# A two-layer diffusion backbone on one core: gate product ahead of the reciprocal, narrower ones in the values, earlier projection blocks, modulation inside attention

## The chip, the cores and the metric

One core of one Trainium2 chip. The time is device microseconds of one execution; the table below gives the median of three runs and the one execution that the hardware profiler took.

## The reference

Two layers over 1024 latent tokens with a prefix of 256 context tokens, model width 1024, all in fp32. Each layer computes a modulation (shift, scale, gate) from a conditioning vector, an RMS norm, one input projection, two parallel mixers with SiLU gates, and one output projection:

```python
def modulation(cond, w, b):
    m = jax.nn.silu(cond) @ w + b
    return jnp.split(m, 3, axis=-1)
...
    for i in range(DEPTH):
        sh_l, sc_l, g_l = modulation(c, mod_w[i], mod_b[i])
        sh_c, sc_c, g_c = modulation(c_ctx, mod_w[i], mod_b[i])
        h_lat = rms_norm(x_lat, norm_g[i]) * (1.0 + sc_l[:, None, :]) + sh_l[:, None, :]
        h_ctx = rms_norm(x_ctx, norm_g[i]) * (1.0 + sc_c) + sh_c
        if i % 2 == 0:
            y_lat, y_ctx = even_mixer(h_lat, h_ctx, ...)   # A: global GQA, B: GQA in a band with a sink
        else:
            y_lat, y_ctx = odd_mixer(h_lat, h_ctx, ...)    # C: conformer convolution, D: 2-D neighbourhood attention
        x_lat = x_lat + g_l[:, None, :] * y_lat
        ...
    return rms_norm(x_lat, final_g)
```

In attention the softmax is followed by the gate: `oa * silu(ag)`, and the same for B and D.

## The kernel before

**Numbers and engines.** Every fp32 operand of a large product is split into a high part (ScalarE cast, line 325) and a low part (the rest, on GpSimd or VectorE, line 328), and a product is three matmuls (lines 347 to 349). TensorE is PE in the profile, VectorE DVE, ScalarE ACT, GpSimd POOL, and SP issues most DMAs.

**Order.** The code emits instructions with priorities, and a scheduler that simulates a timeline sets each engine's order from them. `later(n)` lowers the priority of what is emitted inside it; `issue_after(i)` queues the block's instructions behind `i` on the engine of `i`. `weave(main, n, fill, m)` takes n steps of attention and m of a filling generator in turn.

**Opening.** The string `PLAN` orders it: modulation halves of layer 0 (`a`, `b`, `c` on PE, `v` on DVE), loads of the three token chunks (`0`, `1`, `2`; 256 context tokens, then 512 and 512), sums of squares (`n`), the norm's factor (`r`) and the normalised, modulated and split chunk (`h`, the function `make_h`: line 335 on DVE, lines 338 to 342 on ACT, then the low part on DVE, line 339, or POOL, line 328). After it `fill0(0, w0)` projects the first head group: ten blocks j of 128 tokens with 384 columns (tile `pq`), two to a pair jp, rotary embedding per block (lines 855 to 860), transposes (`qk_tail`, tile `trk`), then three gate blocks (`pg`). The third chunk's norm is woven in at the blocks that `LASTN` names: its sum of squares (`norm_x`, line 726) at block 0, its factor (`norm_bc`, tile `trs`) at block 2, its `h` at block 3. During the opening the flag `solo` is set and the fillers' banks in PSUM (`pp`) come from two tags until `sums` is set, then from one tag with two banks.

**The other modulation halves.** Eight halves of 512 columns are left after `PLAN` (the generator `mod_steps`): the gate part of layer 0 and all of layer 1. A half has nine steps: eight, in each of which 128 rows of the weight are loaded and summed, weighted, on DVE for one or two conditioning vectors (lines 242 and 247; three rows of the second vector go to ACT and POOL), and one that ends it (lines 253 to 258). The first `PSH` halves sum in PSUM (tile `mrun`), the others in SBUF (`macc`). `tick()`, called three times in each projection block, takes one step: at every call while `solo` is set (`TICK0`), then at every third (`TICK1`). While `solo` is set the weights land in the tiles that later hold keys and values (tags KA, KB and V).

**Attention, layer 0.** Four head groups u in the order 2, 3 (B), 0, 1 (A), each in ten query blocks of 128 (a "group" in the code). For a key tile of 128: scores (tile `st`, two banks, lines 503 and 507), exponential (ACT, line 515, tile `pf`, `PFB` = 2 buffers under the tag `ost`), split into `ph` and `pl`, and three tiles later the products with the values (tile `ov`, one bank, lines 445 to 447). The value tile holds for a key tile 64 columns of the low part, 64 of the high part and 64 ones; the ones put the denominator into partitions 64 to 127 of `ov`. A group's end is lines 454 to 459: two transposes of the denominators, the reciprocal, a transpose back, and `finish`: numerators times reciprocals out of PSUM (line 669 in layer 0, 1451 in layer 1), then 0.5 and the gate (671, 1453). The next group's first product needs the bank `ov` and so waits for line 669. Row maxima for the group after next (`mx`, lines 614 to 635) run in between.

While group k runs, the projection of group k+1 fills. In the last one (u = 1) the output projection fills (`out0_part`, tile `po`): first the four features of u = 2, 3, then the two of u = 0, each part with its own accumulation in PSUM and its own addition to x (line 1090). `through_attention` then does the last features.

**Layer 1** has the same attention loop with 16 groups of seven tiles (exponential buffers under the tag `pf`, also `PFB`), beside projections and the output projection. The convolution before it is bound to DVE's line 1200.

## Time and profile before

| | |
|---|---|
| median of 3 runs | 1506.44 us (1504.36 to 1511.38) |
| profiled execution | 1513.41 us, span in the profile 1511.6 us |
| PE busy, granted clock | 1427.4 us, 94% of the span; 0.978 |
| DVE, POOL, ACT busy | 1086.5, 815.9, 750.7 us |
| DMA | 215 MB, mean 142 GB/s |

In a row of the grouped view stand line, engine, operation, output and inputs, shape and count; then the busy time, the mean of one in ns, and the idle time of that engine just before them with what ended it. A matmul's end is modelled, so that two that follow closely overlap in the list; the distance from start to start is the rate.

### The profile page before, as it was taken

The numbers are of one execution on the slowest core, as the hardware profiler recorded it, in microseconds if no ns is written. First come the engines' busy times: TensorE is split into PE (matmuls) and PEld (weight loads), VectorE is DVE, ScalarE is ACT, GpSimd is POOL, SyncE is SP. The second block draws the span as 40 slices with busy tenths as digits, with TensorE's granted clock in tenths as the row PEclk, the third lists the DMA queues.
The fourth block names the chain that finished last, engine by engine and source line by source line (L and its number), as shares of the span: only waits on it lengthen the run. The fifth ranks groups of instructions, "written<-read, shape, count | busy, mean of one in ns | idle before, by whom it ended". The sixth has DMA issues, their size and how long they took to land.

```text
span 1511.6 us, 22035 instructions
## 1 busy us (share of the span) xinstructions
PE 1427.4 (94%) x7006; PEld 1162.7 (77%) x7006; DVE 1086.5 (72%) x2139; ACT 750.7 (50%) x1536; POOL 815.9 (54%) x764
## 2 busy tenths in 40 slices
PE   7699999999999999999999989999999999999996
PEld 2598988887788678778888768888887778777775
DVE  4996787588957677555577686999838467667766
ACT  3541444445453765665455665443444354645563
POOL 3262463466555686776455765754543253354663
PEclk9799999999999999999999989999999999999998
DMA  9766245423541124641111122213596777786523
GB/s 350 260 198 194 70 122 179 143 70 115 159 136 48 45 84 120 221 157 38 49 42 43 60 91 66 92 58 80 164 308 189 206 228 207 249 273 209 190 63 119
DMA packets 182828, 215.24 MB, mean 142 GB/s; under 512 B 17196, under 2 KB 136184, under 8 KB 182712
## 3 DMA queue, kind: packets, MB, share of 16 engines
q1 hardware_dynamic: 172464, 195.97, 41.5%
q10 hardware_dynamic: 10248, 17.87, 3.7%
q8 instruction: 55, 0.90, 0.2%
q14 instruction: 61, 0.50, 0.1%
HBM read 151.64 MB, written 62.13 MB: 141 GB/s over the span
## 4 chain that ended last, share of the span: by engine, by line
PE 68%; DVE 13%; DMA 10%; issue 3%; POOL 2%; SPq 1%; ACT 1%; DVEq 0%; ACTq 0%; POOLq 0%
PE p L347 5%; PE p L348 5%; PE p L349 5%; PE ov L445 4%; PE ov L447 4%; PE ov L446 4%; PE po L347 4%; PE po L349 4%; PE po L348 4%; PE st L507 4%; PE st L503 4%; PE pg L347 2%; PE pg L349 2%; PE pg L348 2%; DMA mw<-in_mod_w_dram 2%
## 5 line engine op out<-in xcount | busy, mean ns | idle before, releaser
L328 POOL TENSOR_TENSOR pl<-pf,ph 128x512 fp32r<-128x512 f32 (+3 forms) x321 | 391.6, 1230 | 263.4 <-ACT ph L325 223.1
L328 POOL TENSOR_TENSOR wl<-wr,wh 128x256 fp32r<-128x256 f32 (+2 forms) x253 | 194.9, 789 | 157.5 <-ACT wh L325 114.6
L515 ACT ACTIVATE pf<-st 128x512 f32<-128x512 f32 x284 | 166.9, 596 | 178.4 <-PE st L507 125.6
L325 ACT CAST ph<-pf 128x512 fp32r<-128x512 f32 (+3 forms) x364 | 206.2, 578 | 25.4 <-PE ov L446 12.7
L347 PE MATMUL p<-hh,wh 128*128 128x512 f32 x448 | 177.9, 399 | 4.8 <-ACT wh L325 3.7
L348 PE MATMUL p<-hl,wh 128*128 128x512 f32 x448 | 178.3, 399 | 0.0
L349 PE MATMUL p<-hh,wl 128*128 128x512 f32 x448 | 173.3, 397 | 0.0
L325 ACT CAST wh<-wr 128x256 fp32r<-128x256 f32 (+2 forms) x260 | 102.0, 404 | 122.8 <-DMA wr<-in_od_d_dram 36.3
L445 PE MATMUL ov<-ph,Vt 128*128 128x512 f32 (+3 forms) x364 | 140.6, 386 | 9.5 <-DVE y L669 6.8
L503 PE MATMUL st<-QH,KAt 128*128 128x512 f32 (+3 forms) x364 | 140.3, 386 | 7.5 <-ACT pf L515 4.3
L447 PE MATMUL ov<-pl,Vt 128*128 128x512 f32 (+3 forms) x364 | 141.6, 391 | 4.9 <-POOL pl L328 3.0
L446 PE MATMUL ov<-ph,Vt 128*64 128x512 f32 (+3 forms) x364 | 138.1, 379 | 0.0
L507 PE MATMUL st<-QL,KBt 68*128 68x512 f32 (+3 forms) x364 | 135.1, 381 | 0.3 <-DVE QL L416 0.3
L1200 DVE SCALAR_TENSOR_TENSOR cps<-U,taps,cps 128x512 f32<-128x512 f32 x184 | 124.3, 749 | 0.1
L627 DVE TENSOR_REDUCE mp<-mx 128x1 f32<-128x512 f32 x128 | 85.6, 685 | 38.6 <-PE mx L626 37.9
L347 PEld LDWEIGHTS p<-hh,wh 128*128 128x128 f32 x448 | 84.6, 189 | 25.6 <-ACT wh L325 4.7
L349 PEld LDWEIGHTS p<-hh,wl 128*128 128x128 f32 x448 | 84.4, 189 | 19.7 <-issue 0.5
L348 PEld LDWEIGHTS p<-hl,wh 128*128 128x128 f32 x448 | 84.6, 189 | 18.9 <-issue 0.2
L447 PEld LDWEIGHTS ov<-pl,Vt 128*128 128x128 f32 x364 | 70.3, 193 | 29.5 <-POOL pl L328 7.8
L445 PEld LDWEIGHTS ov<-ph,Vt 128*128 128x128 f32 x364 | 70.7, 194 | 25.1 <-issue 5.3
L503 PEld LDWEIGHTS st<-QH,KAt 128*128 128x128 f32 x364 | 69.1, 190 | 26.3 <-ACT pf L515 10.3
L347 PE MATMUL pq<-wh,hh 128*128 128x384 f32 x256 | 88.7, 346 | 0.0
(289 smaller groups left out, 3463.5 us busy)
## 6 DMA issues: line engine op xcount, KB each, us to landing
mw<-in_mod_w_dram SPq DMA_DIRECT2D x34, 512.0 KB, 6.0
Q<-qs SPq DMA_DIRECT2D x40, 256.0 KB, 2.6
QH<-Q SPq DMA_DIRECT2D x80, 128.0 KB, 2.8
bm<-in_d_bm_dram SPq DMA_DIRECT2D x16, 540.0 KB, 5.9
wr<-in_od_d_dram SPq DMA_DIRECT2D x64, 128.0 KB, 2.9
mw<-in_mod_w_dram SPq DMA_DIRECT2D x28, 256.0 KB, 3.1
wr<-in_ev_qkv_dram SPq DMA_DIRECT2D x32, 192.0 KB, 4.5
QD<-spq SPq DMA_DIRECT2D x48, 128.0 KB, 2.5
```

The costliest lines, as they stand in the source:

```text
L325: SC.copy(hi, src)
L328: (GP if leng == "g" else VE).tensor_tensor(lo, src, hi.bitcast(F32), op=ALU.subtract)
L347: PE.matmul(o, lh, rh, start=first, stop=False)
L348: PE.matmul(o, lh, rl, start=False, stop=False)
L349: done[0] = PE.matmul(o, ll, rh, start=False, stop=last)
L445: PE.matmul(o, V[:, 64:192], ph, start=(t == 0), stop=False)
L446: PE.matmul(cut(g.ov[0:64], q0, n), V[:, 0:64], ph, start=False, stop=False)
L447: pvs.append(PE.matmul(o, V[:, 64:192], pl, start=False, stop=(last and g.sink is None)))
L503: sts.append(PE.matmul(sf, KA[:, cs], cut(g.QH, q0, n), start=True, stop=False))
L507: PE.matmul(sf, KB[0:68, cs], cut(g.QL[0:68], q0, n), start=False, stop=True)
L515: SC.activation(pf[:, :n], st[:, :n], AF.Exp, scale=1.0 if g.bias else SCALE)
L1200: VE.scalar_tensor_tensor(pc, uc, w, pc, op0=ALU.mult, op1=ALU.add)
```

## The change

- **Group ends.** A new `pre` runs after the two transposes and before the reciprocal: numerator x 0.5 x gate out of PSUM, in two instructions. `finish` multiplies the result by the reciprocals in SBUF.
- **Ones and buffers.** A value tile has 161 columns for a key tile, not 192: 33 ones. The first product of a group still takes 128 columns of weights, the others 97. `PFB` is 3 in both layers.
- **Opening.** `PLAN` gets `q` (blocks 0 and 1 of the first projection, copied to the tile `pc0`) and `n` (the third chunk's sum of squares) ahead of the second chunk's `h`. That sum is halved between POOL and DVE. `LASTN` is (2, 2, 3), with nothing left for the first entry.
- **Modulation.** Ticks count only from block 4; in the opening a step is queued behind the last line 339. `PSH` is 3. `TICK1` is 8, 6 and 16 for the first three head groups. The steps that are left run in u = 1, one at every fifth step of attention from the tenth, in the spare key and value buffers, all sums on DVE.
- **Output projection.** The features of u = 2, 3 and 0 are one part with one accumulation; `O1` is (6, 134, 14).

```diff
-PFB = 2
+VW = 161
+PFB = 3
-PSH = 4
+PSH = 3
-O1 = (6, 84, 46, 14)
-TICK0, TICK1 = (1, 3)
-PLAN = 'pavaa0vabvnabbvabrbbwcVHcccw1Ch2nrh'
-LASTN = (0, 2, 3)
+O1 = (6, 134, 14)
+TICK0, TICK1 = (1, (8, 6, 16))
+PLAN = 'pavaa0vabvnabbvabrbbwcVHcccw1Ch2nrqnh'
+LASTN = (2, 2, 3)
...
+    def new_v(pool, n, bufs):
+        V = pool.tile([P, n * VW + 192 - VW], F32R, tag="V", name=nm("Vt"), bufs=bufs)
+        for k in range(n):
+            GP.memset(V[:, k * VW + P : (k + 1) * VW].bitcast(F32), 1.0)
+        GP.memset(V[:, n * VW :].bitcast(F32), 1.0)
+        return V
...
-            PE.matmul(o, V[:, 64:192], ph, start=(t == 0), stop=False)
-            PE.matmul(cut(g.ov[0:64], q0, n), V[:, 0:64], ph, start=False, stop=False)
-            pvs.append(PE.matmul(o, V[:, 64:192], pl, start=False, stop=(last and g.sink is None)))
+            m = P if t == 0 else VW - 64
+            PE.matmul(o[0:m], V[:, vo + 64 : vo + 64 + m], ph, start=(t == 0), stop=False)
+            PE.matmul(cut(g.ov[0:64], q0, n), V[:, vo : vo + 64], ph, start=False, stop=False)
+            pvs.append(PE.matmul(o[0 : VW - 64], V[:, vo + 64 : vo + VW], pl, start=False, stop=(last and g.sink is None)))
...
+                yu = g.pre(g.ov)
                 VE.reciprocal(r8, r1[:, :, 0])
                 VE.transpose(rb, r8[:, :, None].broadcast_to([P, 8, 32]))
-                g.finish(g.ov, rb)
+                g.finish(yu, rb)
...
-        def finish(ov, rb):
+        def pre(ov):
             y = a0.tile([P, 2, P], F32, tag="y", name=nm("y"), bufs=YB)
             for e in range(2):
                 es = slice(e * 64, (e + 1) * 64)
-                VE.tensor_tensor(y[es], den(ov[0:64, :], e), rb[es, :].rearrange("p (a q) -> p a q", a=2),
-                                 op=ALU.mult)
-            VE.scalar_tensor_tensor(y, y, 0.5, g.gt, op0=ALU.mult, op1=ALU.mult)
+                VE.scalar_tensor_tensor(y[es], den(ov[0:64, :], e), 0.5, g.gt[es], op0=ALU.mult, op1=ALU.mult)
+            return y
+
+        def finish(y, rb):
+            VE.tensor_tensor(y, y, rb.rearrange("p (a q) -> p a q", a=2), op=ALU.mult)
...
+                if c == 2:
+                    both_ = []
+                    for k, eng in enumerate((GP, VE)):
+                        acc = kvp.tile([P, 512], F32, tag="QH", name=nm("acc"), bufs=3)
+                        for dk in range(4 * k, 4 * k + 4):
...
+                                eng.tensor_tensor(acc[:, :n], acc[:, :n], sq[:, :n], op=ALU.add)
...
+                elif ev == "q":
+                    pc0.append(a0.tile([P, NTOK], F32, tag="KB", ...)[:, 0:768].rearrange("p (j n) -> p j n", j=2))
+                    for j in range(2):
+                        pp = bank("pp", nm("pq0"))
+                        for dk in range(DK):
+                            mm3(pp[:, :384], Hs(h, 0, j * P, P, dk), Hs(h, 1, j * P, P, dk), w0[0][dk], w0[1][dk], ...)
+                        SC.copy(pc0[0][:, j, :], pp[:, 0:384])
...
-        def tick():
+        def tick(gate_=False):
+            if late[0]:
+                return
             beat[0] += 1
-            if beat[0] % (TICK0 if solo[0] else TICK1) == 0:
+            if beat[0] % (TICK0 if solo[0] or unit[0] < 0 else TICK1[unit[0]]) == 0:
...
+                    if solo[0]:
+                        with tc.issue_after(hend[0].ins):
+                            mod_next()
...
-        run(mods)
+        while mdone[0] < 18 or mdone[0] % 9:
+            mod_next()
...
+        def paced():
+            steps_[0] += 1
+            if steps_[0] == 10:
+                spare_tiles()
+            if steps_[0] >= 10 and (steps_[0] - 10) % 5 == 0:
+                with later(LATE), tc.issue_after(redl[0].ins):
+                    mod_next()
+        hook[0] = paced
...
-        parts = [[2 * u + k for u in sorted(us) for k in range(2)] for us in (ORDER[:2], ORDER[2:3], ORDER[3:])]
+        parts = [[2 * u + k for u in sorted(us) for k in range(2)] for us in (ORDER[:3], ORDER[3:])]
+        parts[0] = [f for f in parts[0] if f // 2 != ORDER[2]] + [f for f in parts[0] if f // 2 == ORDER[2]]
...
-        weave(main, O1[0], load_oh(parts[0]), 6, False)
-        weave(main, O1[1], out0_part(parts[0]), 48, False)
-        weave(main, O1[2], chain(load_oh(parts[1]), out0_part(parts[1])), 30, False)
+        weave(main, O1[0], load_oh(parts[0]), 9, False)
+        weave(main, O1[1], with_mods(out0_part(parts[0]), 1000), 72, False)
+        hook[0] = None
+        run(mods)
```

In layer 1 `pre` and `finish` are changed in the same way, with a tile `yu` of 128 x 256 between them.

More of the change, by code (lines that the diff above doesn't have):

```diff
@@ L112, in tile_kernel @@
     turn = [0, 0]
-    mk, mwp, hold, layer = [0], [None], [0], [0]
+    mk, mwp, hold, layer, spare = [0], [None], [0], [0], []
     sums, made_v = [False], [0]
@@ L198, in mod_half @@
             yield
-        row = a0.tile([P, 512], F32, tag="ost", name=nm("mrow"), bufs=2)[0:2, :]
+        row = a0.tile([P, 512], F32, tag="ost", name=nm("mrow"), bufs=PFB)[0:2, :]
         SC.copy(row, pb[0:2, :])
@@ L218, in mod_half_v @@
         pool, tag, bufs = (kvp, "QH", 3) if mwp[0] is not None else (pool, "macc", 2)
-        accs = [pool.tile([P, 512], F32, tag=tag, name=nm("macc"), bufs=bufs) for _ in conds]
+        if spare:
+            accs = spare[0][: len(conds)]
+        else:
+            accs = [pool.tile([P, 512], F32, tag=tag, name=nm("macc"), bufs=bufs) for _ in conds]
         runs = accs
@@ L242, in mod_half_v @@
                     VE.tensor_scalar(r_, w, csil[:, dk, q : q + 1], None, op0=ALU.mult)
-                elif dk in MODP[q] and not solo[0]:
+                elif dk in MODP[q] and not solo[0] and not spare:
                     SC.activation(w, w, AF.Identity, scale=csil[:, dk, q : q + 1])
@@ L328, in split, with after_h @@
         (GP if leng == "g" else VE).tensor_tensor(lo, src, hi.bitcast(F32), op=ALU.subtract)
+    hend = [None, None]
+    @contextmanager
+    def after_h():
+        with tc.issue_after(hend[0].ins), tc.issue_after(hend[1].ins):
+            yield
     def make_h(l, c, xs, bc, h, dks=range(DK)):
@@ L376, in v_tiles @@
     def v_tiles(pool, n, bufs=1):
-        Vs[:] = [pool.tile([P, n, 192], F32R, tag="V", name=nm("Vt"), bufs=bufs) for _ in range(bufs)]
-        for V in Vs:
-            GP.memset(V[:, :, 128:192].bitcast(F32), 1.0)
+        Vs[:] = [new_v(pool, n, bufs) for _ in range(bufs)]
     def k_tiles(pool, n, bufs=1):
@@ L537, in weave @@
             next(main, None)
+            if hook[0] is not None:
+                hook[0]()
             while done * nmain < (k + 1) * nfill:
@@ L680, in group0 @@
         hs = (u - 2) * 4
-        g = Group(load_q=load_q, start=lambda: None, last=last, bias=False, ahead=lambda t: None, rate=3 if isb else 2, gate=gate, v=lambda k: V0s[u][:, k, :], load_v=None, maxes=maxes, nmp=1 if qb < 2 else (2 if isb else 3),
+        g = Group(load_q=load_q, start=lambda: None, last=last, bias=False, ahead=lambda t: None, rate=3 if isb else 2, gate=gate, v=lambda k: (V0s[u], k), load_v=None, maxes=maxes, nmp=1 if qb < 2 else (2 if isb else 3),
                   sink=(sink[:, hs : hs + 4], sink8[:, hs : hs + 4]) if isb else None, skm=lambda: sk, k=lambda: (KAs[u], KBs[u]),
-                  tiles=[(k, 0, 512, x) for k, x in kt], den=den, finish=finish)
+                  tiles=[(k, 0, 512, x) for k, x in kt], den=den, pre=pre, finish=finish)
         g.prep = attn_prep(kvp, g)
@@ L730, in norm_bc @@
                 n = CHUNKS[c][1]
-                return run(rstd_steps(pool, [acc], n, "st"))[:, :n]
-            made = [0]
+                return run(rstd_steps(pool, acc if c == 2 else [acc], n, "st"))[:, :n]
+            made, pc0 = [0], []
             accs, bcs = [], []
@@ L868, in proj_qkv @@
                             step()
-                pc = ap.tile([P, 2, 384], F32, tag="pc", name=nm("pc"), bufs=PCB)
+                pc = pc0[0] if w and jp == 0 else ap.tile([P, 2, 384], F32, tag="pc", name=nm("pc"), bufs=PCB)
                 for jj in range(2):
+                    if w and jp == 0:
+                        continue
                     j = 2 * jp + jj
@@ L875, in proj_qkv @@
                                 step()
+                    if w and j == 4:
+                        late[0] = 0
                     pp = bank("pp", nm("pq"))
@@ L959, in tile_kernel @@
         while hold[0]:
-            next(mods)
+            mod_next()
         assert not tails
@@ L1066, in load_oh @@
                     x1.append(op_.tile([P, DK, n], F32, tag=f"x1_{c}", name=nm("x1"), bufs=1))
-                for f in range(f0, f1, 2):
+                for f in fs[::2]:
                     lo = oh[c][1][:, f : f + 2, :]
@@ L1445, in den, with pre, finish @@
                 return dn[:, k * 256 : (k + 1) * 256].rearrange("p (a q) -> p a q", a=2)
-            def finish(ov, rb):
+            def pre(ov):
+                yu = dpool.tile([P, 256], F32, tag="yu", name=nm("yu"), bufs=1)
+                for k in range(2):
+                    VE.scalar_tensor_tensor(yu[k * 64 : (k + 1) * 64], ov[0:64, k * 256 : (k + 1) * 256], 0.5,
+                                            g.gt[ds, k * 256 : (k + 1) * 256], op0=ALU.mult, op1=ALU.mult)
+                return yu
+            def finish(yu, rb):
                 fin[0] += 1
```

86 lines of the change are left out of this document (61 added, 25 removed).

## The prediction

> **What bounds the kernel now.** I read the page first, then the busy times by stage, then who made PE wait, then the opening in order of time.
>
> ```profile
> span 1511.6 us, 22035 instructions
> PE 1427.4 (94%) x7006; PEld 1162.7 (77%) x7006; DVE 1086.5 (72%) x2139; ACT 750.7 (50%) x1536; POOL 815.9 (54%) x764
> PE 68%; DVE 13%; DMA 10%; issue 3%; POOL 2%; SPq 1%; ACT 1%; DVEq 0%; ACTq 0%; POOLq 0%
> ```
>
> PE is busy for 94% of the span, so at most 1511.6 - 1427.4 = 84 us can go while the number of matmuls stays. The stages (columns: window, its length, then busy time and count of PE, weight load, DVE, ACT, POOL, then granted clock, DMA share, GB/s):
>
> ```profile
> 0.00:63.00 63.00, 40.09 (x148) 17.41 (x148) 41.88 (x84) 32.00 (x65) 20.34 (x25) 0.92 0.94 333
> 63.00:135.00 72.00, 68.64 (x399) 65.16 (x400) 64.50 (x121) 22.08 (x51) 31.75 (x33) 0.93 0.67 204
> 135.00:385.00 250.00, 239.40 (x1248) 205.02 (x1246) 191.15 (x425) 113.17 (x262) 131.09 (x111) 0.99 0.40 117
> 500.00:640.00 140.00, 132.44 (x609) 101.28 (x608) 93.44 (x170) 89.52 (x160) 102.84 (x78) 0.98 0.39 118
> 640.00:840.00 200.00, 199.46 (x946) 159.39 (x945) 125.82 (x227) 105.79 (x197) 116.60 (x102) 1.00 0.22 68
> ```
>
> PE idles 22.9 us before 63, 3.4 from 63 to 135, 10.6 in the B attention (135 to 385), 7.6 where the A attention begins (500 to 640), and 0.5 in all of 640 to 840. From 63 to 135 DVE is as full (64.5 of 72) as PE. Who made PE wait over the whole span (total, times, longest), with one wait of ACT behind them:
>
> ```profile
> PE trs L279 <- DVE acc L726: 13.0, 1, 13.0
> PE ov L445 <- DVE y L669: 6.8, 6, 2.2
> PE st L503 <- ACT pf L515: 4.3, 9, 1.2
> ACT pf L515 <- POOL pl L328: 37.0, 44, 3.2
> ```
>
> One wait in the opening is as long as the next several together; the change's three parts aim at these three rows of PE.
>
> **The change part by part.** Sums are made against the profiled execution, 1513.4 us, which lies 7.0 us above the median of 1506.4.
>
> *Opening.* The long wait in order of time:
>
> ```profile
> 49.27 1.16 PE L290 MATMUL bc<-ident,nr 128*128 128x128 f32 x8 [0.75 <-POOL nr L265]
> 51.63 5.35 DVE L335 SCALAR_TENSOR_TENSOR xr<-xr,gs,bc 128x512 f32<-128x512 f32 x8
> 54.37 3.73 POOL L328 TENSOR_TENSOR hl<-xr,hh 128x512 fp32r<-128x512 f32 x3 [5.15 <-ACT hh L325]
> 56.90 0.75 DVE L247 SCALAR_TENSOR_TENSOR mrun<-mw,csil,mrun 128x512 f32<-128x512 f32 x1
> 57.55 1.10 DVE L726 TENSOR_TENSOR acc<-acc,sq 128x512 f32<-128x512 f32 x1
> 58.58 0.74 DVE L247 SCALAR_TENSOR_TENSOR mrun<-mw,csil,mrun 128x512 f32<-128x512 f32 x1
> 59.58 0.85 ACT L884 COPY pc<-pq 128x384 f32<-128x384 f32 x2
> 59.75 2.35 POOL L328 TENSOR_TENSOR hl<-xr,hh 128x512 fp32r<-128x512 f32 x1 [1.65 <-ACT hh L325]
> 60.90 0.74 DVE L247 SCALAR_TENSOR_TENSOR mrun<-mw,csil,mrun 128x512 f32<-128x512 f32 x1
> 62.57 0.68 DVE L726 TENSOR_TENSOR acc<-acc,sq 128x512 f32<-128x512 f32 x1
> 63.17 0.74 DVE L339 SCALAR_TENSOR_TENSOR hl<-xr,modT,hh 128x512 fp32r<-128x512 f32 x1
> 63.40 1.84 PE L279 MATMUL trs<-ones,acc 128*128 128x2 f32 x8 [12.97 <-DVE acc L726]
> 65.10 0.67 PE L347 MATMUL pq<-wh,hh 128*128 128x384 f32 x1
> ```
>
> Three things hold PE between 50.4 and 65.1. The third chunk's sum of squares is queued on DVE among the second chunk's `h` and the modulation sums, and `trs`, which needs it, stands in PE's queue in front of block 2. The context blocks' two banks are copied out only at 59.6. And the last low part of the second chunk comes at 63.9. The edit moves all three: `n` stands ahead of `h` and three of its six additions go to POOL, which is idle from 49.2 to 54.4; `q` copies the banks out earlier; and no modulation sum stands between 51 and 64 (three here, 2.2 us, and two additions, 1.8 us). Then the last low part on DVE comes near 63.9 - 4.0 = 59.9 and POOL's fourth at 59.75 + 2.35 = 62.1 or a little earlier. PE can begin block 2 with the first low parts (54.4 plus a third of 3.73 = 55.6) and follow them, so when the last one is there, most of blocks 2 and 3 lies behind it. Before, these began at 65.1, the first matmuls at 0.67 us each. I count blocks 2 and 3 as ending 11 us earlier: the 13.0 less 2 for the following. Late next is DVE, and it decides how much stays. In the opening 39 steps of modulation ran, 30 in ten blocks and 9 in the gates; now 18 + 9 = 27. Eight of nine steps carry two sums:
>
> ```profile
> L247 DVE SCALAR_TENSOR_TENSOR mrun<-mw,csil,mrun 128x512 f32<-128x512 f32 x48 | 33.6, 745 | 0.0
> L247 DVE SCALAR_TENSOR_TENSOR macc<-mw,csil,macc 128x512 f32<-128x512 f32 x51 | 44.1, 885 | 25.8 <-DMA mw<-in_mod_w_dram 24.4 <-POOL macc L245 1.2
> ```
>
> 12 x 8/9 x 2 x 0.745 = 15.9 us of DVE leave the opening. That is more than 11, so DVE's own end moves as far as PE's; but the 27 steps (35.8 us) now begin only after the third chunk's `h`, and KA, KB and V are handed to attention only behind them. Ends: 16 us (all of DVE's relief) and 2 us (the hand-over comes as late as before). I take 11, which is nearer to the PE row. The early blocks themselves add no matmul, and their copy out of PSUM was there before. The loads of the 12 steps leave a stretch in which DMA is at 0.67 to 0.94.
>
> *Third exponential buffer.* PE waits 4.3 us for a bank of scores that ACT hasn't read, because ACT waits for a buffer (37.0 us, 44 times, mostly off the path). With a third buffer ACT runs a tile further ahead. POOL's own rate is unchanged, and so the wait can move to the `ph` and `pl` buffers: ends 0 and 4.3 (more only if a wait spoils the spacing behind it); I take 3.5, by the row. 33 ones instead of 64 pay for the space. The memsets for them go from one for a tile to eleven on POOL, once in the opening and once in layer 1; I count 1 us.
>
> *Group ends.*
>
> ```profile
> L455 DVE STREAM_TRANSPOSE r<-ov 64x256 f32<-64x256 f32 x112 | 50.7, 453 | 14.6 <-PE ov L447 10.8 <-PE ov L450 1.7
> L457 DVE RECIPROCAL r<-r 128x8 f32<-128x8 f32 x56 | 11.1, 198 | 0.7
> L458 DVE STREAM_TRANSPOSE rb<-r 128x256 f32<-128x256 f32 x56 | 24.6, 439 | 0.8
> L669 DVE TENSOR_TENSOR y<-ov,rb 64x256 f32<-64x256 f32 x80 | 33.1, 414 | 1.1
> L671 DVE SCALAR_TENSOR_TENSOR y<-y,gt 128x256 f32<-128x256 f32 x40 | 24.0, 600 | 0.6
> L1540 DVE SCALAR_TENSOR_TENSOR x<-po,modT,xs 128x256 f32<-128x256 f32 x32 | 14.0, 475 | 12.4 <-PE po L349 9.1 <-DMA xs<-X 3.2
> ```
>
> Before, the bank is free after 2 x 0.453 + 0.198 + 0.439 + 2 x 0.414 = 2.37 us of DVE. Now after 2 x 0.453 + 2 x 0.475 (two tensors and a factor out of PSUM, the nearest row) = 1.86: 0.51 earlier. PE waited for this 6 times, so 3.1 us; ends 0 (other DVE work gets in between) and 6.8 (the waits go wholly). DVE's sum per end is the same within 0.2 us. The gate must land 1.4 us earlier; it is issued half a group ahead. I take 3.
>
> *Modulation in attention.* Steps in the B attention fall from 33 to 7 + 8 = 15 (57 ticks by 8, 48 by 6), so 18 x 8/9 x 2 = 32 sums of 0.885 = 28 us leave 250 us, in which DVE is busy for 191 and PE idles 10.6. A good half of that idle time isn't in the two rows counted already; I take 3, ends 0 and 6. Three steps go to u = 0, and 27 (three halves: 16 + 8 + 8 = 32 sums, 28.3 us) to 640 to 840.
>
> ```profile
> L1090 DVE SCALAR_TENSOR_TENSOR x<-po,modT,x 128x512 f32<-128x512 f32 x48 | 35.8, 748 | 33.2 <-PE po L349 32.9
> L1090 DVE SCALAR_TENSOR_TENSOR x<-po,modT,x 128x256 f32<-128x256 f32 x24 | 11.2, 474 | 7.3 <-PE po L349 7.2
> ```
>
> There the joined output part drops a third of these rows, 16 x 0.748 + 8 x 0.474 = 15.8 us. DVE rises from 125.8 to 138 of 200 us. The cover is DVE's slack, and PE has none to lose: 0 if it holds, up to 28.3 if each sum delays a row maximum. Loads of u = 0's output now stand at the start of u = 1 behind its last write, on SP's queue, and `through_attention` has 28 steps for what had 32. For these together I count 1 us.
>
> *Narrow weights.* 308 + 364 products take 97 columns instead of 128. A 64-column load stands in the trace already:
>
> ```profile
> L445 PEld LDWEIGHTS ov<-ph,Vt 128*128 128x128 f32 x364 | 70.7, 194 | 25.1 <-issue 5.3 <-ACT ph L325 4.3 <-DVE y L669 3.0
> L446 PEld LDWEIGHTS ov<-ph,Vt 128*64 128x64 f32 x364 | 50.3, 138 | 11.3
> 705.23 0.39 PE L445 MATMUL ov<-ph,Vt 128*128 128x512 f32 x1
> 705.46 0.40 PE L446 MATMUL ov<-ph,Vt 128*64 128x512 f32 x1
> 705.69 0.40 PE L447 MATMUL ov<-pl,Vt 128*128 128x512 f32 x1
> ```
>
> It takes 138 ns, and its matmul still starts 0.23 us after the one before and is followed after 0.23. So the moving side sets the rate, and I count 0. The Trainium skill, page "TensorE: Matmul & The Clock Gate", sections "LDWEIGHTS" and "Back-to-back issue gap", has the load proportional to the columns (P / 1.2 ns) and says that the spacing is "set by both ops"; by that an estimate of 31 / 1.2 = 26 ns on 672 products would bring 17 us more. The trace agrees with the first, not with the second at 512 moving columns.
>
> *Sum.* 11 + 3.5 + 3 + 3 - 1 - 1 = 18.5 us. 1513.4 - 18.5 = 1494.9; with the 7.0 us to the median, 1488.
>
> **The rivals.**
>
> *The opening hands its gain back.* The modulation steps start late, all at once, and attention waits for KA and V. For it speaks that DVE is 90% busy from 63 to 135; against it the 15.9 us that leave. The opening then gives 2: 1506.4 - 9.5 = 1497.
>
> *Little of it arrives.* The waits on buffers and banks turn into waits on POOL (102.84 of 140 us at 500 to 640), the opening gains 2 to 5, and the moved work takes the rest: 1503.
>
> *Narrow weights speed PE up.* A load of 64 columns takes 138 ns and one of 128 takes 194, so 31 columns fewer are worth 27 ns; if each of 672 products saved that, 18 us more would go: 1470. The spacing at 705 us speaks against it.
>
> *Slower: the moved sums sit in front of the row maxima in u = 1.* Place: 640 to 840, where PE idles 0.5 us. Price: 28.3 us if PE waits out each sum. It decides once 32 sums cost more than 18.5 + 7.5 us, 0.8 of each one's 0.885. Then 1506.4 - 18.5 + 28.3 = 1516. Against it: 62 us of free DVE time, and low priority.
>
> **How the numbers follow.** 0.5% (7.5 us) is about what a measurement of this kernel tells from no change. Forecast 0.64 (its own range 1477 to 1496), first rival 0.12, second 0.11, narrow weights 0.05, slower 0.08. Faster, below 1499: 0.64 + 0.05 + most of the first rival, 0.09 = 0.78; slower 0.07, above 1514; same 0.15. The range reaches from 1472, near the case of narrow weights, to the second rival (1503).
>
> **What would show it.** The wait of `trs` before 63 us falls from 13.0 to under 3, and block 2's rotary products come some 10 us earlier. ACT's 37.0 us behind `pl` fall by half or more; PE's wait for `y` falls below 4. From 640 to 840 PE stays above 198 of 200. 97-column products keep 0.23 us from start to start. Wrong if PE idles at the hand-over near 120 us, or if row maxima in u = 1 wait behind modulation sums.

## The result, and the profile after

The changed kernel takes 1491.3 us, the median of six runs (1488.7 to 1494.9); the kernel before took 1507.2 in six runs beside it. The ratio is 0.989, with a 95% interval of 0.987 to 0.991: 15.9 us less, where 18.5 were forecast (1488, range 1472 to 1503). The profiled execution of the changed kernel took 1491.75 us, 21.7 less than that of the kernel before. The latter, 1513.4, lies above all six timed ones (1504.4 to 1511.4), so some 6 us of the 21.7 belong to that execution and not to the change.

The head of the page, and the shares of the chain that ended last:

```profile
span 1490.0 us, 22025 instructions
PE 1419.0 (95%) x7014; PEld 1146.4 (77%) x7014; DVE 1069.9 (72%) x2126; ACT 739.1 (50%) x1537; POOL 821.8 (55%) x802
PE 74%; DVE 8%; DMA 7%; issue 4%; POOL 4%; ACT 2%; SPq 0%; DVEq 0%; POOLq 0%; ACTq 0%
```

PE's idle time fell from 84.2 to 71.0 us, and its busy time from 1427.4 to 1419.0 with the same work (the eight matmuls more are those of `trs`, two columns wide, which now adds two partial sums). The second part has another cause than the first; the opening shows it below. The stages by time, with the columns of before:

```profile
0.00:63.00 63.00, 49.52 (x186) 26.60 (x187) 37.36 (x76) 32.05 (x66) 26.71 (x29) 0.94 0.93 326
63.00:135.00 72.00, 69.08 (x396) 63.49 (x395) 57.60 (x107) 22.18 (x51) 32.73 (x54) 0.98 0.62 187
135.00:385.00 250.00, 245.18 (x1308) 211.54 (x1308) 184.05 (x432) 121.36 (x284) 137.99 (x120) 1.00 0.37 112
500.00:640.00 140.00, 132.94 (x626) 100.73 (x626) 97.64 (x169) 85.30 (x158) 102.09 (x78) 0.99 0.45 140
640.00:840.00 200.00, 198.00 (x953) 156.03 (x953) 138.63 (x235) 99.93 (x193) 115.82 (x97) 1.00 0.28 84
```

PE gains 9.4 us of busy time before 63 us and 5.8 in the B attention, where the granted clock is now 1.00 throughout. The waits that answer to those of before (total, times, longest):

```profile
PE ov L472 <- DVE y L700: 4.2, 5, 1.4
PE ov L472 <- DVE yu L1546: 3.4, 2, 2.5
PE ov L474 <- POOL pl L337: 2.6, 7, 0.7
PE st L531 <- ACT pf L543: 0.9, 2, 0.7
ACT pf L543 <- POOL pl L337: 13.1, 11, 2.7
```

The wait of 13.0 us for `acc` is gone, and PE's wait for exponentials fell from 4.3 to 0.9. ACT's wait behind POOL's low parts fell from 37.0 to 13.1. The wait for `y` fell from 6.8 to 4.2, and a wait for `yu`, the group end of layer 1, has come. The opening in order of time, at the place where `trs` stood for 13 us:

```profile
47.65 0.51 PE L365 MATMUL pq<-wh,hc 128*128 128x384 f32 x2
49.98 1.16 PE L299 MATMUL bc<-ident,nr 128*128 128x128 f32 x8 [1.83 <-POOL nr L274]
51.61 3.70 PE L288 MATMUL trs<-ones,acc 128*128 128x2 f32 x16 [0.47 <-POOL acc L762]
55.17 0.67 PE L363 MATMUL pq<-wh,hh 128*128 128x384 f32 x1
56.28 0.52 PE L364 MATMUL pq<-wl,hh 128*128 128x384 f32 x1
56.60 0.52 PE L365 MATMUL pq<-wh,hl 128*128 128x384 f32 x1
59.07 0.34 PE L365 MATMUL pq<-wh,hl 128*128 128x384 f32 x1
59.24 0.34 PE L363 MATMUL pq<-wh,hh 128*128 128x384 f32 x1
61.54 0.44 PE L365 MATMUL pq<-wh,hl 128*128 128x384 f32 x1 [1.78 <-POOL hl L337]
```

Block 2 begins at 55.17 instead of 65.10. Its matmuls of 384 columns start 0.32 us apart at 56.3 and 0.17 apart at 59.1, with nothing waited for: the first run at half the clock. So this stall cost twice, once while PE stood and once more while it ran again. In the trace the granted clock has two values only, 1.0 and 0.5, and 0.5 comes in multiples of 3.41 us. The profiled execution of before had 66 us of half rate in its span, that of the changed kernel 32.

**PE time lost.** The time from one matmul's start to the next one's, less what that distance is at full rate with no wait (231 ns at 512 columns, 174 at 384, 118 at 256), holds both: idle time and half rate. Summed over consecutive matmuls of the trace it can be compared between kernels, since the full-rate distances add up to the same 1326 us, within 0.5 us, in every kernel here. Stages are cut where PE's work says so: the first score product (143.4 us before, 128.5 after), the first of the third unit (u=0), the first of the fourth (u=1), the last score product of layer 0, the first and the last of layer 1.

```
PE time lost (us)        opening  B units   u=0   u=1   boundary  layer 1  tail    sum   ratio to before
before                      42.5     29.1    20.6   7.7      24.5     37.0  11.0  172.4
changed                     32.7     17.3    20.4   8.3      28.3     33.0  11.0  151.0   0.989
```

The difference, 21.4 us, is the difference of the spans (21.6). It lies in two stages: 9.8 in the opening and 11.8 in the B units. (The full-rate distance of the smallest products, of 128 columns and fewer, is less certain; with other values for it the two come out as low as 7.7 and 10.2.) The first score product comes 14.9 us earlier: beside the 9.8, 43 matmuls fewer stand ahead of it (546 for 589; 5.1 us at full rate). The rest of the kernel gives +0.2 in sum. Each row of this table is one execution, so the 6 us above are in it, and it can't be told in which stage.

### The profile page after: what moved, and what is told of

Its sections match the earlier page's. It is cut to its first block, busy times and chain, and to the rows that moved or that the text cites. A ratio compares the mean times of both kernels' runs of the same rounds, so it can differ in the third digit from the quotient of the medians.

```text
span 1490.0 us, 22025 instructions
## 1 busy us (share of the span) xinstructions
PE 1419.0 (95%) x7014; PEld 1146.4 (77%) x7014; DVE 1069.9 (72%) x2126; ACT 739.1 (50%) x1537; POOL 821.8 (55%) x802
## 4 chain that ended last, share of the span: by engine, by line
PE 74%; DVE 8%; DMA 7%; issue 4%; POOL 4%; ACT 2%; SPq 0%; DVEq 0%; POOLq 0%; ACTq 0%
PE p L363 7%; PE p L365 7%; PE p L364 7%; PE ov L472 4%; PE ov L474 4%; PE st L531 4%; PE ov L473 4%; PE st L535 4%; PE po L363 4%; PE po L365 3%; PE po L364 3%; PE pq L365 3%; PE pq L363 3%; PE pq L364 3%; PE pg L363 2%
## 5 line engine op out<-in xcount | busy, mean ns | idle before, releaser
L472 PE MATMUL ov<-ph,Vt 128*97 128x512 f32 (+4 forms) x364 | 138.4, 381 | 12.7 <-DVE y L700 4.2
L474 PE MATMUL ov<-pl,Vt 128*97 128x512 f32 (+3 forms) x364 | 138.4, 381 | 5.2 <-POOL pl L337 2.6
L363 PEld LDWEIGHTS p<-hh,wh 128*128 128x128 f32 x448 | 84.2, 188 | 23.1 <-ACT wh L334 2.0
L365 PEld LDWEIGHTS p<-hh,wl 128*128 128x128 f32 x448 | 84.2, 188 | 20.7 <-POOL wl L337 1.0
L364 PEld LDWEIGHTS p<-hl,wh 128*128 128x128 f32 x448 | 84.2, 188 | 20.0 <-issue 0.5
L365 PE MATMUL pq<-wh,hl 128*128 128x384 f32 x256 | 87.8, 344 | 1.8 <-POOL hl L337 1.8
L364 PE MATMUL pq<-wl,hh 128*128 128x384 f32 x256 | 88.3, 345 | 0.0
L472 PEld LDWEIGHTS ov<-ph,Vt 128*97 128x97 f32 (+1 forms) x364 | 60.9, 167 | 32.4 <-issue 8.2
```

The costliest lines, as they stand in the source:

```text
L363: PE.matmul(o, lh, rh, start=first, stop=False)
L364: PE.matmul(o, lh, rl, start=False, stop=False)
L365: done[0] = PE.matmul(o, ll, rh, start=False, stop=last)
L472: PE.matmul(o[0:m], V[:, vo + 64 : vo + 64 + m], ph, start=(t == 0), stop=False)
L474: pvs.append(PE.matmul(o[0 : VW - 64], V[:, vo + 64 : vo + VW], pl, start=False, stop=(last and g.sink is None)))
```

## Experiments

Times are given as ratios to the kernel before, run beside each on the same chip, with a 95% interval; 0.001 is 1.5 us. The table of lost PE time for all of them stands at the end of this section.

### One part put back: the opening

```
-PLAN = 'pavaa0vabvnabbvabrbbwcVHcccw1Ch2nrqnh'; LASTN = (2, 2, 3); PSH = 3
+PLAN = 'pavaa0vabvnabbvabrbbwcVHcccw1Ch2nrh';   LASTN = (0, 2, 3); PSH = 4
-(norm_x halves the third chunk's squares, pc0, late, issue_after(hend))
+(as before)
```

> The changed kernel with the opening put back as before: no early context blocks, all eight squares of the third chunk added on DVE behind the second chunk's h, modulation steps from the first block on (33 to 39 of them before attention instead of 27). Theory: the opening is the largest part and its lead stays to the end: 11 to 15 us slower than the changed kernel (1491.3), so 1502 to 1506, with the trs wait of about 13 us back. Rival: the hand-over to attention eats the lead, because with more steps done early there are fewer later: at most 4 us slower, 1491 to 1495, though the wait is back.

Ratio 1.0052 (1.0034 to 1.007): 24 us slower than the changed kernel, more than either theory. The wait is back:

```profile
PE trs L288 <- DVE acc L759: 12.9, 1, 12.9
```

In the opening the loss is 42.1 us, 9.4 more than in the changed kernel, as expected. But the B units lose 28.9 for 17.3, u=0 loses 4.6 more and u=1 6.6 more, where nothing of the opening runs. In u=1 only 8 modulation sums stand here, against 32 in the changed kernel, so its loss there isn't theirs.

### One part put back: the pacing of the modulation

```
-TICK0, TICK1 = (1, (8, 6, 16))
+TICK0, TICK1 = (1, (3, 3, 3))
-        while mdone[0] < 18 or mdone[0] % 9: mod_next()
+        run(mods)
-        hook[0] = paced
```

> The changed kernel with the modulation inside attention paced as before (a step every third tick in all three units, the rest run out before u=1, none in u=1); the opening keeps its 27 steps. Theory: the 12 us by which PE's stalls in the B attention fell (27.5 to 15.3 us between 135 and 385) come mainly from the sums that left: 5 to 8 us slower than the changed kernel, 1496 to 1499. As predicted: 3 us, 1494. Rival: the stalls fell for the third buffer and the group ends, and the sums were beside the path: within 1.5 us, 1490 to 1493.

1.0105 (1.0089 to 1.0121): 32 us slower than the changed kernel. All of it lies in the B units, which lose 56.0 us for 17.3. The rival falls; the theory had the place right and the size wrong by a factor of five. PE idles 21.4 us there for 4.8, and 37.5 us are at half rate, where the changed kernel has none; its waits for row maxima rise from 1.2 to 8.5 us.

### One part put back: two exponential buffers

```
-PFB = 3
+PFB = 2
```

> The changed kernel with two exponential buffers instead of three; value tiles stay narrow. Theory (the prediction's term): 3.5 us slower, 1495, with ACT's wait behind POOL's low parts back at some 30 us and PE's wait for exponentials at 3 to 5 us. Rival 1: the wait only moves to the high and low parts' buffers: within 1 us of 1491.3. Rival 2: the buffer is what emptied the B attention of stalls: 6 to 10 us slower, 1497 to 1501.

1.0041 (1.0019 to 1.0064): 23 us slower than the changed kernel. The waits are back where they were foretold, and beyond:

```profile
ACT pf L543 <- POOL pl L337: 29.0, 35, 2.3
PE st L531 <- ACT pf L543: 9.6, 7, 3.3
```

The B units lose 6.6 us more, and layer 1, whose scores use the same number of buffers, 14.9 more. PE's wait for exponentials is 3.2 us in the former and 3.3 in the latter, where the changed kernel has none; the rest of the 14.9 is mostly half rate (27.3 us for 3.4).

### One part put back: the group ends

```
-                yu = g.pre(g.ov)
                 VE.reciprocal(r8, r1[:, :, 0])
                 VE.transpose(rb, r8[:, :, None].broadcast_to([P, 8, 32]))
-                g.finish(yu, rb)
+                g.finish(g.ov, rb)     # numerator by reciprocal from PSUM, then the gate, in both layers
```

> The changed kernel with the group ends of before in both layers: reciprocal and second transpose first, then numerator by reciprocal out of PSUM, then the gate. Theory (the prediction's term): 3 us slower, 1494. Rival 1: the waits for y in layer 0 come back, but those for yu in layer 1 (7 to 8 us by the changed kernel's list) are new and go: within 1 us of 1491.3 or up to 2 us faster. Rival 2: 5 to 7 us slower, 1497 or more.

0.9966 (0.9953 to 0.998): 11 us slower than the changed kernel. 6.5 of the lost time is in the B units, 13.3 in u=1; u=0 and the boundary each lose 2.6 to 2.8 less, and layer 1 the same. The theories allowed for 3, for next to nothing, and for 5 to 7 us or more. But the wait that all of them are about didn't come back. PE's longest wait for row maxima, and the one for `y`:

```profile
PE mx L656 <- DVE mp L657: 6.3, 8, 2.7
PE ov L472 <- DVE y L699: 1.7, 2, 1.4
```

With the group ends of before, PE waits 1.7 us for `y` and 0.6 in layer 1, where the changed kernel waits 4.2 and 3.4. What rose are its waits for row maxima, from 2.5 to 14.4 us in sum, and half rate, from 32 to 66.

### Nothing put back: other layouts of the same work

The four parts cost 24, 32, 23 and 11 us: 90 together, while the whole change brought 16. A planner orders the instructions by simulated time, and each of these edits also made it order the rest anew: in layer 1, whose code the opening doesn't touch, PE's instructions stood in another order after the opening was put back. So two variants of the changed kernel were run that change the order, and one of the kernel before. The first adds and moves no work; the other two also load one constant of 2 KB earlier.

```
changed:  -LATE = 100
          +LATE = 90                                   (n_after_late90)
changed and before: dwb = const("dwb", [P, 4])  moved to the start   (n_after_dwb, n_before_dwb)
```

> The changed kernel with one number changed, the planner's priority offset of the modulation steps (LATE 90 for 100). No work is added, moved between engines or taken away; the order in which PE's instructions stand differs in the first three eighths of the kernel and in the seventh. Theory (the four undone parts cost 14 to 34 us each, 99 us together against a gain of 16, because each also made the planner lay out the rest of the kernel anew, and PE's short stalls in a new layout set off half-rate windows of the clock): this one too is slower than the changed kernel, by 5 to 20 us, with 10 to 35 us more of half-rate time. Rival (each undone part cost what it cost by itself): within 3 us, ratio to before 0.987 to 0.991.

0.9955 (0.9934 to 0.9975), 10 us slower than the changed kernel. Half rate rose by 12.5 us, and 11.6 us of the lost time are in the B units (28.9).

> The changed kernel with one 2 KB constant (a bias that only layer 1 uses) loaded at the start instead of before u=1. The order differs only from the middle on (PE in eighths 5 to 7). Theory of the new layout: 3 to 15 us slower than the changed kernel, and the loss lies behind 640 us, none before. Rival: within 3 us.

0.9933 (0.9911 to 0.9954), 6 us slower. The B units lose 18.1, as expected of an order that is the same there; u=1 loses 3 more, in the same order as well, and layer 1 loses 6 more.

> The kernel before with the same 2 KB constant loaded at the start; PE's order differs in the first half. Theory of the new layout: the kernel before is not at a chance low or high, so the time moves by up to 15 us either way, more than 4 us in absolute value. Rival: ratio to before 0.997 to 1.003.

1.0105 (1.0079 to 1.0131), 16 us slower than the kernel before, with 83 us of half rate for 66.

So edits that leave the work as it is move this kernel by 6 to 16 us, and a total can't price a part of 3 us. The lost time of one stage is a better measure, but only where the order is the same. By the traces, PE's instructions stand in one order in the B units of five kernels: the changed one, `dwb` early, and three of those below (128 columns, sums doubled, sums on ACT and POOL). These lose 17.3 to 18.7 there. With `LATE` at 90 the order is another, and they lose 28.9: a new order alone cost 11.6. Each of the four kernels with a part put back has another order in the B units too. So a loss there far above 12 us is the part's (the pacing's 38.7), while the 6.6 of the buffers and the 6.5 of the group ends may be the order's. In the opening, where most of these kernels have one order, the scatter is smaller: all eleven kernels with the new opening lose 31.0 to 34.6.

The theory of layouts holds. It doesn't explain all: three of the four parts put back cost more than any layout did.

### Value products at 128 columns

```
-            m = P if t == 0 else VW - 64
-            PE.matmul(o[0:m], V[:, vo + 64 : vo + 64 + m], ph, ...)
+            PE.matmul(o, V[:, vo + 64 : vo + 192], ph, ...)      (and the third product alike)
```

> The changed kernel with all value products at 128 columns again (the tiles stay 161 columns wide; the extra columns are the neighbour key tile's and fall in rows that nothing reads). As predicted (the moving side sets the rate): spacing stays at 0.23 us, and where the order of instructions stays the same (PE in the first three eighths) the time to there is the same within 1 us. Rival (the spacing follows the load too): 672 products at 21 to 27 ns each are 14 to 18 us slower, spread over both layers. A difference behind 500 us, where the order changes, is the layout's.

0.9928 (0.9904 to 0.9952), whose interval overlaps the changed kernel's. Up to the third unit, where the order is the same, it loses 32.5 + 18.7 us for 32.7 + 17.3. The loads did get longer, by form (count, busy us, mean ns), first the changed kernel, then this one:

```profile
L474 PEld LDWEIGHTS ov<-pl,Vt 128*97 128x97 f32 x364 | 59.6, 164 | 27.0 <-POOL pl L337 7.7 <-DVE pl L337 3.3
L473 PEld LDWEIGHTS ov<-ph,Vt 128*64 128x64 f32 x364 | 49.4, 136 | 15.6
```

```profile
L473 PEld LDWEIGHTS ov<-pl,Vt 128*128 128x128 f32 x364 | 69.1, 190 | 29.1 <-POOL pl L337 9.6 <-DVE pl L337 3.0 <-issue 0.6
```

26 ns for each of 672 products, and PE doesn't feel it: over the 852 value products of 512 columns, the median distance from start to start is 232 ns in the changed kernel and 233 here. In the changed kernel's order of time, products of 97, 64 and 97 columns and their neighbours:

```profile
700.00 0.40 PE L472 MATMUL ov<-ph,Vt 128*97 128x512 f32 x1
700.24 0.40 PE L473 MATMUL ov<-ph,Vt 128*64 128x512 f32 x1
700.47 0.39 PE L474 MATMUL ov<-pl,Vt 128*97 128x512 f32 x1
700.70 0.39 PE L472 MATMUL ov<-ph,Vt 128*97 128x512 f32 x1
700.92 0.39 PE L531 MATMUL st<-QH,KAt 128*128 128x512 f32 x1
```

All start 0.22 to 0.24 us apart. The rule of the Trainium skill that the prediction weighed (page "TensorE: Matmul & The Clock Gate", section "Back-to-back issue gap": the spacing is set by both operations) isn't borne out with 512 moving columns.

### Parts added to the kernel before

The opening alone:

> The kernel before with the new opening alone (early context blocks, the third chunk's squares halved between POOL and DVE and put ahead of h, modulation steps only from the fifth block on); everything behind is as before, so 12 modulation steps more than before fall into attention at a step every third tick. Theory A (the opening is nearly the whole gain, the other parts are within the layout's scatter): the first score product comes 14 to 17 us earlier than before and the lead stays, 1490 to 1498. Theory B (opening and pacing belong together: the steps that leave the opening clog DVE in attention unless they go on to u=1, as the changed kernel with the old pacing showed at 300 to 485 us): the hand-over comes 14 to 17 us earlier, but 5 to 20 us of it are gone by the end of the B attention, 1500 to 1512.

1.0191 (1.0177 to 1.0204): 29 us slower than before, worse than either theory. The first score product comes 13.0 us earlier, at 130.4, and the start of the third unit 8.5 us later. The B units of before, and then of this kernel (start and end, length, then busy time and count of PE, weight load, DVE, ACT, POOL, granted clock):

```profile
143.38:463.43 320.05, 308.44 (x1613) 264.81 (x1612) 243.83 (x534) 151.49 (x339) 172.54 (x144) 0.99 0.41 121
```

```profile
130.36:471.91 341.55, 328.72 (x1662) 281.29 (x1660) 250.80 (x548) 154.96 (x345) 175.44 (x149) 0.96 0.39 118
```

21.5 us longer, of which the 49 matmuls more explain 5.9; 15.6 us are lost PE time, and the clock fell to 0.96. PE's idle time rose by 1.2 us only, from 11.6 to 12.8; nearly all of the loss is half rate, 30.7 us for 3.4. What changed there by intent is the modulation. The accumulating sums on DVE in these two stretches, before and with the new opening:

```profile
L247 DVE SCALAR_TENSOR_TENSOR macc<-mw,csil,macc 128x512 f32<-128x512 f32 x33 | 31.4, 960 | 19.4 <-DMA mw<-in_mod_w_dram 18.1 <-POOL macc L245 1.2
```

```profile
L247 DVE SCALAR_TENSOR_TENSOR macc<-mw,csil,macc 128x512 f32<-128x512 f32 x43 | 39.5, 933 | 20.8 <-DMA mw<-in_mod_w_dram 20.5
L242 DVE TENSOR_SCALAR macc<-mw,csil 128x512 f32<-128x512 f32 x8 | 4.1, 516 | 4.0 <-DMA mw<-in_mod_w_dram 4.0
```

With the four that open an accumulation (eight in the second kernel), 37 became 51: the steps that the opening no longer does. In front of them DVE also stands idle for weights (18.1 us in all before; now 20.5, and 4.0 for the eight that open an accumulation). Row maxima stand between the sums in DVE's queue, and PE's waits for them in this stretch rose from 2.8 to 6.3 us. The two longest rows:

```profile
PE mx L636 <- DVE mp L637: 2.7, 2, 1.8
PE mx L616 <- DVE mp L637: 2.7, 1, 2.7
```

Two of the five half-rate stretches begin behind such a wait (1.8 and 2.7 us); the others begin behind waits for other results of DVE, POOL and ACT (0.7 to 1.4 us). So the path from the sums to the half rate is seen in part, and for the rest it is argued. The size isn't sure either, since another order alone cost 11.6 us in these units.

The opening and the pacing together:

> The kernel before with the new opening and the new pacing of the modulation (27 steps in the opening, 18 in the units before u=1, 27 in u=1); two exponential buffers, 128-column value products, the old group ends and three output parts. Theory A and B both: the gain of the whole change within the layout's scatter of 5 to 15 us, 1488 to 1502, hand-over 14 to 17 us earlier. Rival (third buffer and group ends carry 6 to 7 us, as predicted): 1496 to 1500, and PE's waits for exponentials and y are as long as before (4.3 and 6.8 us).

1.0046 (1.0029 to 1.0064), 22 us faster than the opening alone, and slower than every theory had it. The same row now, and the B units:

```profile
L254 DVE SCALAR_TENSOR_TENSOR macc<-mw,csil,macc 128x512 f32<-128x512 f32 x20 | 19.8, 1014 | 22.2 <-DMA mw<-in_mod_w_dram 22.2
```

```profile
130.16:456.93 326.77, 313.07 (x1626) 268.11 (x1625) 234.78 (x516) 153.49 (x342) 174.08 (x146) 0.99 0.35 108
```

24 sums for 51, and 31.2 us lost for 44.7. PE's idle time there didn't fall (13.7 us for 12.8), nor did DVE's in front of the sums (22.7 for 24.5). What fell is half rate, from 30.7 to 3.4 us, and PE's waits for row maxima, from 6.3 to 1.0. The waits for exponentials (5.5) and for `y` (6.3) are as long as before. Theory A, that the opening is nearly the whole gain, falls; theory B is right that the two belong together, but in this order they don't bring the gain without the other parts.

### The moved sums doubled

```
                     VE.scalar_tensor_tensor(t if dk == DK - 1 else r_, w, csil[...], r_, ...)
+                    if spare:
+                        VE.scalar_tensor_tensor(t, w, csil[...], t, ...)
```

> The changed kernel with each of the 28 modulation sums of u=1 that accumulate done twice (the second one spoils layer 1's modulation values, so the output differs): 25 us more of DVE between 640 and 850. Theory, as predicted (the sums stand in DVE's slack): PE stays above 196 of 200 us busy from 640 to 840 and the time within the layout's scatter, 1490 to 1500. Rival (they stand in front of the row maxima): 15 to 25 us slower, 1506 to 1516, with PE waiting for mp or for acc's followers between 640 and 850.

0.9982 (0.9966 to 0.9998): 14 us slower than the changed kernel, between the two. The unit u=1 of before, of the changed kernel and of this one:

```profile
665.40:874.63 209.23, 207.05 (x977) 165.00 (x976) 135.48 (x242) 112.74 (x211) 121.42 (x102) 0.99 0.15 48
```

```profile
638.42:852.55 214.13, 212.13 (x1029) 167.37 (x1028) 145.86 (x249) 111.34 (x215) 127.72 (x108) 1.00 0.29 87
```

```profile
637.58:860.60 223.02, 215.45 (x1022) 167.00 (x1021) 173.91 (x277) 114.32 (x216) 133.79 (x108) 0.99 0.27 84
```

The length alone misleads: the changed kernel's unit is 4.9 us longer than that of before because 52 more matmuls lie in it; PE idles 2.2 us in the one and 2.0 in the other. With the sums doubled it idles 7.6, and the lost time goes from 8.3 to 17.6: by that 0.33 us for each of 28 sums, a third of what one takes on DVE. The order in u=1 is another here, though, and the kernel with 128 columns, which has the 32 sums as they were, lost 13.0 there in another order. So how much of the 9.3 is the sums' stays open. PE's waits for row maxima are 1.0 us in this unit, and 2.2 for `y`.

### Twelve of the moved sums on ACT and POOL

```
-                elif dk in MODP[q] and not solo[0] and not spare:
+                elif not solo[0] and dk in ((1, 3, 5, 6) if spare and q == conds[-1] else () if spare else MODP[q]):
```

> The changed kernel with 12 of the 32 modulation sums of u=1 taken from DVE and done as a scaled copy on ACT and an addition on POOL. So far unit u=1 (from its first score product to the next unit's end) took 207 to 211 us without moved sums, 214 to 220 with 32 and 223 with 60. Theory (the moved sums cost about 0.2 to 0.3 us each, because they stand on DVE between the row maxima): u=1 takes 2 to 4 us less than with 32, 211 to 215, and the time is 1486 to 1494 unless the layout of layer 1 takes it back. Rival (POOL, at 116 of 200 us, delays the low parts instead): u=1 takes 218 us or more and PE's wait for POOL's pl grows from 2.6 to over 6 us; 1496 to 1502.

0.9915 (0.9898 to 0.9931), which overlaps the changed kernel's interval; the unit took 215.9 us and lost 9.3 for 8.3. Neither theory holds. The 16 accumulating sums left on DVE take 1.22 us each, where the 28 took 0.94. PE idles 1.9 us in the unit, as before (2.0): a wait of 1.4 us for ACT's `ph` is gone, and the wait for POOL's low parts rose from 0.2 to 1.5. Over the whole kernel it is:

```profile
PE ov L474 <- POOL pl L337: 5.6, 8, 1.3
```

It was 2.6. No kernel here beats the changed one.

### Lost PE time of all kernels

```
PE time lost (us)        opening  B units   u=0   u=1   boundary  layer 1  tail    sum   ratio
before                      42.5     29.1    20.6   7.7      24.5     37.0  11.0  172.4
 + dwb early                49.1     34.3    24.0   7.7      24.5     31.2  11.0  181.8   1.0105
 + opening                  31.3     44.7    30.8   7.2      25.0     45.0  11.0  195.0   1.0191
 + opening, pacing          31.8     31.2    19.6   8.6      25.2     42.8  10.8  170.0   1.0046
changed                     32.7     17.3    20.4   8.3      28.3     33.0  11.0  151.0   0.989
 - opening                  42.1     28.9    25.0  14.9      24.5     34.2  10.7  180.3   1.0052
 - pacing                   34.0     56.0    18.0   4.3      25.2     37.4  10.7  185.5   1.0105
 - third buffer             31.2     23.9    21.3  11.9      27.6     47.9  11.0  174.7   1.0041
 - group ends               33.1     23.8    17.8  21.6      25.5     33.3  11.0  166.3   0.9966
 LATE 90                    31.0     28.9    19.4   8.4      24.3     39.3  10.7  161.9   0.9955
 dwb early                  34.6     18.1    20.4  11.4      24.4     39.0  10.7  158.6   0.9933
 128 columns                32.5     18.7    18.9  13.0      27.1     32.2  10.7  153.1   0.9928
 moved sums doubled         31.9     18.1    19.8  17.6      27.5     37.2  10.7  162.8   0.9982
 12 sums on ACT, POOL       32.8     18.3    20.5   9.3      24.8     40.2  11.0  156.9   0.9915
```

## Why the prediction was right, point by point

The forecast sum was 18.5 us against the profiled execution of before (1513.4); the profiled execution after is 21.7 lower, and the medians differ by 15.9. The total was right. That it agrees so well is in part luck: the 21.7 hold some 6 us of one execution, layouts of the same work lie 6 to 16 us apart, and in the B units a cost that the sum lacks and gains larger than its terms nearly cancel. The opening is shown, by its wait and by all kernels with and without it. The terms of the B units are right in sum and not shown singly.

*Opening, 11.* Right, mechanism and size. In its stage the pair gives 9.8; the three kernels with the old opening lose 44.6 on average and the eleven with the new one 32.4, so 12.1. Block 2 came 9.9 us earlier, as forecast ("some 10"). The following of the low parts is there too: PE stands 1.78 us for `hl` at 61.5, where 2 were allowed.

*The steps that leave the opening: a missing term.* The prediction let 15.9 us of DVE leave the opening and asked whether attention would start late (the first rival). It doesn't. The price falls a stage later: with 14 more sums on DVE the B units lose 15.6 us more when the pacing stays as it was, nearly all of it at half rate. Part of this can be the new order. The rival that the opening hands its gain back was right in kind, and wrong in place and condition.

*Modulation moved out of the B attention, 3 (ends 0 and 6): the mis-sized step.* With the new opening the new pacing is worth 13.5 us in the B units (44.7 to 31.2), and 38.7 with all other parts in place (17.3 to 56.0). Both are far above the term, and the second far above what an order cost. The working priced sums by their busy time and by PE's idle time in the kernel before. It left out the half rate behind stalls: 30.7 us of it in the B units with the opening alone, 3.4 with the pacing too. It also left out DVE's idle time in front of the sums, which the quoted row had (24.4 us behind the DMA); but that time stayed when the pacing came (24.5 and 22.7 us), so it isn't what the pacing saved. Its count was off as well: it took two DVE sums for each of 18 steps, 32; by the traces 37 became 24, since late steps carry one condition and some second conditions go to ACT and POOL.

*Third buffer, 3.5 (ends 0 and 4.3).* By its own wait, right: PE waits for exponentials 4.3 to 9.6 us in the five kernels with two buffers (6.7 in the mean) and 0.9 to 5.5 in the nine with three (3.0). By lost time more came back than the upper end, 6.6 in the B units, though in another order. In layer 1 the three kernels with the new opening and two buffers lose 42.8 to 47.9, the eight with three buffers 32.2 to 40.2. With the old opening two buffers lose no more there (31.2 and 37.0, against 34.2), so the layer 1 part depends on the layout.

*Group ends, 3 (ends 0 and 6.8).* Not shown, and the wait that the term was priced by speaks against it. PE's wait for group ends (`y`, and `yu` in layer 1) is 1.0 to 6.8 us in the five kernels with the old ends and 5.2 to 10.2 in the nine with the new ones. In layer 0 alone it is 4.1 and 4.5 in the mean; in layer 1 it is 0 to 0.6 with the old ends and 2.0 to 3.7 with the new ones, which was not foreseen. So the fall from 6.8 to 4.2 in this pair (below 4 was forecast) can be a matter of the order. The step that isn't borne out is that a bank free 0.51 us earlier shortens each wait by as much. Why the old ends put back cost 6.5 in the B units and 13.3 in u=1 stays open; the order differs in both.

*How these add up.* In the B units: 29.1 before, +15.6 by the opening, -13.5 by the pacing, -13.9 by the rest, 17.3 after. So -11.8 in sum, against the 9.5 of the three terms. The single steps hold the cost or gain of a new order each, and the agreement of the sum is no proof of the terms.

*Moved sums in u=1, 0.* Held for this kernel: DVE rose to 138.63 of 200 us (138 was forecast), PE was busy for 198.00 (199.46 before; "above 198" was forecast), and the unit lost 8.3 us for 7.7. How thick the cover is can't be read from these runs: without moved sums and with all other parts the unit lost 4.3, with the sums doubled 17.6, but with the same 32 sums and all parts it lost 8.3 to 13.0, by order and execution. The slower rival, each sum in front of a row maximum, isn't borne out: PE waits 1.0 us for row maxima there with the sums doubled.

*Memsets, -1.* 38 small ones take 2.8 us on POOL where 4 took 2.3: nothing. *Output part, -1.* The boundary loses 3.8 more than before, but 24.3 to 28.3 over the layouts of the same edits. The joined output part wasn't put back by itself, so its share stays open. *Narrow weights, 0.* Right, and the rival at 1470 with it gone. One reading beside it is wrong: the trace doesn't show the load proportional to the columns. Loads of 64, 97 and 128 columns take 136, 164 and 190 ns, about 0.84 ns for each column and some 82 besides.

Open is also why the old opening with all else new loses 28.9 in the B units, with only 21 sums there: its order is another, and by size it could be that, as with `LATE` at 90.

## What to carry to other kernels

Price a stall by its length and by the half rate behind it. When work is taken out of one stage, name the stage in which it lands and price it there; one part may only pay with the other. When a part is meant to shorten a wait, look for that wait when the part is put back: a slower kernel alone doesn't show that the wait was the reason. Where a planner lays out the order, measure how far an edit that changes nothing moves the time, and do so for each stage that is to be read. Then read single parts from the lost time of their own stage, at equal matmuls, and only where they stand clear of that.

## What the runs showed of the hardware

In these traces the half rate goes with PE's idle share of a window, and not with one long gap. The clock's changes lie on a grid of 3.41 us. Over the 14 profiled executions, by the idle share of a full-rate window of that grid, the next window was at half rate this often:

```
idle share    below 30%   30-40%   40-50%   50-60%   60% and more
windows            5554      121       69       51             52
then half rate        6       14       25       43             52
```

The longest single gap in the windows that tipped (were followed by half rate) was below 3 us in all but two of 140. Such a stretch in the changed kernel, at the layer boundary (the same columns as above):

```profile
857.50:860.70 3.20, 0.71 (x2) 0.22 (x2) 3.20 (x6) 3.17 (x6) 1.18 (x1) 1.00 0.00 0
860.70:864.10 3.40, 3.27 (x14) 3.17 (x15) 3.40 (x4) 0.62 (x1) 2.90 (x2) 0.50 0.09 24
864.10:870.90 6.80, 3.29 (x26) 2.88 (x25) 6.50 (x18) 1.54 (x4) 0.82 (x3) 1.00 0.03 10
870.90:874.30 3.40, 3.40 (x9) 2.66 (x10) 0.74 (x2) 2.34 (x7) 2.07 (x3) 0.50 0.00 0
```

PE is busy for 0.71 of 3.20 us, then half the clock; half busy for two windows, then half the clock again, in which 9 matmuls fill 3.40 us. The Trainium skill, page "TensorE: Matmul & The Clock Gate", section "Part 1: The HAM clock gate", has the window of 3413 ns and the two rates, with which the traces agree. Its rule in "HAM oscillation" is to avoid idle gaps over about 3.4 us; here windows tipped that were about half idle, with gaps of 1 to 2.5 us, so here the idle share of a window is the better guide.
